# Filters and spectra of the long convolutions in column-scaled half-precision pairs, transform matrices used as loaded

## The chip, the cores and the metric

The kernel runs on one core of one Trainium2 chip. The core has five engines with a queue of instructions each: TensorE (PE in the profile; its weight loads are PEld), VectorE (DVE), ScalarE (ACT), GpSimd (POOL) and SyncE (SP), which here only issues transfers. The metric is the device time of one execution in microseconds (us), the median of three runs.

## The reference, cut to what matters

The model has two layers over 1024 latent tokens and 256 context tokens of width 1024. The first layer sends half of the channels through a Fourier transform, the other half through a gated long convolution (Hyena, order 2), whose filters come from a small network over positions:

```
def hyena_filters(L, w1, b1, freq, w2, b2, w3):
    ...
    h = jnp.sin(freq * (z @ w1 + b1))
    h = jnp.sin(freq * (h @ w2 + b2))
    h = (h @ w3).reshape(L, 2, HY_ORDER, HY_CH)
    ...
    h = h * jnp.exp(-t01 * deltas)[:, None, None, :]
    h = h / jnp.sum(jnp.abs(h), axis=(0, 1), keepdims=True)
    fwd, bwd = h[:, 0], h[:, 1]
    return jnp.concatenate([fwd, jnp.zeros_like(fwd[:1]), bwd[:0:-1]], axis=0)

def long_conv(u, filt, skip):
    ...
    ff = jnp.fft.rfft(filt, n=2 * L, axis=0)
    y = jnp.fft.irfft(uf * ff[None], n=2 * L, axis=1)[:, :L]
    return y + u * skip
```

Each column (channel, order) of the filter is divided by its own sum of absolute values, so a factor on a column of `w3` drops out of the result. There are two orders of 512 channels, and the filters are made for both lengths, 1024 ("l") and 256 ("c"), from the same weights. The second layer is neighbourhood attention; both layers end in a gated feed-forward part.

## The kernel before

One core does everything in one pass; activations lie with channels on the 128 partitions and tokens along the free axis, in tiles of 512 tokens. The program is written as Python generators whose steps are interleaved by hand; a planner then fixes the order on each engine from its own model of the instruction times, with buffers taken from pools of a fixed number of slots (20 of 4 KB per partition, 34 of 2 KB, two each of the tags `ws`, `wh`, `wl`, and eight banks of PSUM). An instruction queued behind a waiting one on its engine waits with it.

What is computed before the first projection:

- `filter_mlp` makes the hidden layer of the filter network for both lengths at once (640 columns), with a range reduction on VectorE before each sine, and splits the result into a rounded part and a remainder (`ta`, `tb`).
- `ada_first` (64 four-byte matmul instructions) makes two of the six modulations of layer 0 from sixteen 512 KB blocks of `ada_k`, loaded from POOL's queue into `wh`/`wl`.
- `filter_raw` loads the two directions of `w3` for an order, forms their sum and difference (L621), splits each into a high and a low part (helper `split`, L287 on ScalarE and L289 on VectorE), multiplies with `ta`/`tb` block by block, and multiplies the PSUM result with a decay tile `win` (L641), which SP loads in the step that uses it.
- `filter_spectrum` turns the raw filter of an order into its spectrum: four transform families i, four blocks b each. The nested generator `operands` combines the raw halves (L702 to L708), splits the combination, and fetches the transform matrix with `cmat`: a half-precision pair is loaded into a staging tile (tag `ws`) and cast on ScalarE (L335) to a four-byte tile (`wh`/`wl`). For every block and each of four output tiles, three matmuls follow: high × high, high × low, low × high. At the end of a family four PSUM tiles are evicted by ScalarE (L745) and stored by SP.
- `filter_sum`, advanced from within `filter_spectrum`, sums the absolute values over positions: two absolute values on ScalarE (L653, L654), a maximum (L655) and a running addition (L657) on VectorE, and 1-column matmuls that add over partitions.
- `norms` squares the rows of x and the context (ten 512 KB loads from SP, L2144), and normalises the transposed blocks (L550 to L553) as operands of the projection.

The order at the start: one step each of the network, the adaLN generator, the raw filter of order 0 and the norms, then the rest of the network, eight steps of adaLN, and the raw filter, whose VectorE and ScalarE instructions in its next step are tied behind the network's last clamp and sine. Raw filter 1 runs under spectrum 0, the norms under spectrum 1. Then `in_proj` begins; under its sixteen blocks run the 256-token filters (the same functions with "c", the sums and differences there on POOL) and 32 further adaLN steps.

Of the kernel before, what the change touches and what calls it, by code (L numbers as in the profile page):

```python
# [10 lines left out]
F32 = mybir.dt.float32  # L11
F32R = mybir.dt.float32r
F16 = mybir.dt.float16
# [188 lines left out]
class Builder:  # L202
# [117 lines left out]

    def cmat(self, w, src, view=None, small=False, shift=False):

        if small:
            st, m = self.S2(F16), self.S2(F32R, w)
            self.ld(view(st[:, :w]) if view else st[:, :w], src)
            self.nc.scalar.copy(m, st[:, :w])
            return m
        st = self.pw.tile([P, w], F16, tag="ws", name=self.nm("cs"))
        self.ld(view(st) if view else st, src)
        if shift:  # L330
            self.mk ^= 1
            m = self.shifted(("wh", "wl")[self.mk], "mat", w)
        else:
            m = self.mat(w)
        self.nc.scalar.copy(m, st)  # L335
        return m
# [224 lines left out]
    def filter_mlp(self):  # L561
# [12 lines left out]
        for layer, w in enumerate((w1, w2)):  # L574
            s = self.S4(F32, 640)
            for c0, cw in ((0, 512), (512, 128)):
                ps = self.PS()
                self.mm(ps[:, :cw], w, x[:, c0:c0 + cw], True, True)
                nc.vector.tensor_scalar(s[:, c0:c0 + cw], ps[:, :cw], vec[:, layer:layer + 1], vec[:, 2:3],
                                        op0=ADD, op1=MUL)  # L580
            n = self.S4(F32, 640)
# [6 lines left out]
            x = s  # L588
        self.tap("mlp", x)
        self.ta, self.tb = {}, {}  # L590
        for sq, c0, cw in (("l", 0, 512), ("c", 512, 128)):
            ta, tb = self.S2(F32R, cw), self.S2(F32R, cw)
            cs = slice(c0, c0 + cw)
            nc.scalar.copy(ta[0:64], x[0:64, cs])
            nc.vector.tensor_tensor(ta[64:128], x[0:64, cs], ta[0:64].bitcast(F32), SUB)
            nc.scalar.copy(tb[64:128], x[64:128, cs])
            nc.vector.tensor_tensor(tb[0:64], x[64:128, cs], tb[64:128].bitcast(F32), SUB)
            self.ta[sq], self.tb[sq] = ta, tb
        self.sgn = self.S2(F32R)
        self.ldr(self.sgn, a["sgn"][:, :512])  # L600
        self.alt = self.C(4, F32R)
# [3 lines left out]
        self.frg, self.rn, self.kap = {}, {}, {}  # L605

    def filter_raw(self, sq, raws, os=(0, 1)):
# [3 lines left out]
        w3, st = {}, {}  # L611
        for o in os:
            for j in (0, 1):
                st[(o, j)] = self.S2()
                self.ld(st[(o, j)], a["w3"][:, (2 * j + o) * HC:(2 * j + o + 1) * HC])
        if sq == "l":
            yield
        for o in os:
            for eo, op in ((0, ADD), (1, SUB)):
                t = self.T()  # L620
                (nc.vector if sq == "l" else nc.gpsimd).tensor_tensor(t, st[(o, 0)], st[(o, 1)], op)  # L621
# [23 lines left out]
    def filter_sum(self, sq, o, raw):  # L645
# [3 lines left out]
        if sq == "l":  # L649
            acc = self.S4()  # L650
            for b in range(nb):
# [4 lines left out]
                if b:  # L656
                    nc.vector.tensor_tensor(acc, acc, t, ADD)  # L657
# [21 lines left out]
    def filter_spectrum(self, sq, o, raw):  # L679
# [8 lines left out]
        fh = (self.S2(F32R), self.S2(F32R))  # L688
        nc.scalar.copy(fh[0][0:1, :], re[0:1, :])
        nc.vector.tensor_tensor(fh[1][0:1, :], re[0:1, :], fh[0][0:1, :].bitcast(F32), SUB)  # L690
# [5 lines left out]
        def operands():  # L696
            for i in range(4):
                for b in range(nb):
# [1418 lines left out]
    def run(self):  # L2117
# [11 lines left out]
        def drain(g):  # L2129
            for _ in g:  # L2130
                pass
# [60 lines left out]
        next(ng)  # L2192
        drain(mlp)
# [313 lines left out]
```

## Time and profile before

| | us |
|---|---|
| median of three runs | 2925.82 |
| the three runs | 2924.45 to 2926.82 |
| profiled execution | 2922.39 |
| its span | 2920.6 |
| mean granted clock of TensorE | 0.98 |

How to read it: the page lists the busy time of each engine, then the costliest groups of instructions, one line each: line of the kernel, engine, operation, output <- inputs with their shapes, count, busy time, mean duration in ns, and behind the second bar the engine's idle time just before them with what ended it ("releaser"). The timeline lists instructions in order of time: start, duration, instruction, and in brackets the idle time before. The list of waits says which engine waited for what: total, number, longest. The table by stretches gives, for each stretch from the span's start, the busy time of PE, PEld, DVE, ACT and POOL with the number of instructions, the granted clock of TensorE as a share of full speed, the share of the transfer engines and GB/s. Four-byte matmul operands, f32 and its faster form fp32r, both show as f32 on TensorE's rows.

### The profile page before, as it was taken

To read this page: it belongs to the slowest core of one execution; us is meant where nothing else is said; L and a number is where in the kernel's file an instruction comes from. 1 tells how busy PE (TensorE), PEld (TensorE's weight loads), DVE (VectorE), ACT (ScalarE), POOL (GpSimd) and SP (SyncE) were. 2 spreads that over 40 slices of the span, in tenths; PEclk is the share of its full clock that TensorE was granted. 3 is DMA by queue.
4 is the path that set the end of the run, shared out by engine and by line. 5 is a ranking of instruction groups with operands and counts; after the bars stand their busy time and mean duration, and the time that the engine had idled before them with its cause. 6 is when DMAs were issued, how large, how long until landed. Compare 5 with 4: busy or idle time off the path is not lost. (4 is left out here: it accounts for less than half of the span.)

```text
span 2920.6 us, 46051 instructions
## 1 busy us (share of the span) xinstructions
PE 2777.4 (95%) x16163; PEld 1710.9 (59%) x16163; DVE 2094.0 (72%) x3833; ACT 1647.9 (56%) x2899; POOL 641.4 (22%) x1057
## 2 busy tenths in 40 slices
PE   7889999999989999999999999999999999999998
PEld 3766557878879644444555844677665444444554
DVE  5678867585367798877886777777676778775765
ACT  4675325453675666654555555677664477654553
POOL 1012013354220111123120012454443022112000
PEclk9999999999999999999999999999999999999999
DMA  7574435358685555565995798777775666425753
GB/s 263 182 272 161 156 123 158 110 160 287 257 348 192 207 209 195 201 218 218 332 332 174 267 343 296 171 188 180 184 198 187 238 226 232 152 94 183 237 193 115
DMA packets 325156, 615.98 MB, mean 211 GB/s; under 512 B 90934, under 2 KB 130552, under 8 KB 324922
## 3 DMA queue, kind: packets, MB, share of 16 engines
q1 hardware_dynamic: 252378, 384.38, 40.4%
q0 software_dynamic: 70240, 224.45, 21.5%
q10 hardware_dynamic: 2304, 4.20, 0.4%
q8 instruction: 127, 2.08, 0.3%
q14 instruction: 107, 0.88, 0.1%
HBM read 455.33 MB, written 135.53 MB: 202 GB/s over the span
## 5 line engine op out<-in xcount | busy, mean ns | idle before, releaser
L1444 PE MATMUL ps<-s,s 128*128 128x512 f16 x2592 | 583.2, 382 | 15.8 <-ACT tk L1449 7.2
L1444 PEld LDWEIGHTS <-s 128*128 128x128 f16 x2640 | 258.9, 98 | 334.6 <-issue 30.3
L283 PE MATMUL ps<-s,wh 128*128 128x256 f32 (+3 forms) x1752 | 395.7, 329 | 13.1 <-ACT wh L287 7.3
L1213 ACT ACTIVATE s<-s,c 128x512 f16<-128x512 f32 (+1 forms) x324 | 233.3, 753 | 137.9 <-DMA s<-d 75.8
L1661 PE MATMUL ps<-s 128*128 128x512 f16 (+2 forms) x1308 | 305.0, 379 | 2.0 <-DVE s L1214 2.0
L1214 DVE SCALAR_TENSOR_TENSOR s<-s,c,s 128x512 f16<-128x512 f32 (+1 forms) x324 | 247.4, 794 | 78.3 <-ACT s L1213 77.7
L283 PE MATMUL pq<-s,wh 128*128 128x512 f16 (+1 forms) x1000 | 282.0, 356 | 12.2 <-DMA wh<-d 4.7
L283 PEld LDWEIGHTS <-wh 128*128 128x128 f16 x1664 | 160.3, 99 | 172.7 <-issue 24.7
L283 PE MATMUL ps<-s,wl 128*128 128x256 f32 (+3 forms) x876 | 260.2, 330 | 1.0 <-DVE wl L289 0.9
L274 POOL DMA_DIRECT2D d<-s x201 | 109.0, 543 | 660.5 <-DVE s L1505 193.1
L1661 PEld LDWEIGHTS <-s 128*128 128x128 f16 x1536 | 148.7, 98 | 179.5 <-issue 7.1
L283 PE MATMUL ps<-s,s 128*128 128x65 f16 (+5 forms) x2666 | 220.5, 235 | 20.2 <-DMA s<-s 8.2
L335 ACT CAST mat<-cs 128x1024 fp32r<-128x1024 f16 (+2 forms) x120 | 111.6, 935 | 139.0 <-PE ps L283 56.7
L283 PEld LDWEIGHTS ps<-s,wh 128*128 128x128 f32 x1088 | 178.0, 193 | 20.0 <-ACT wh L287 8.3
L283 PE MATMUL ps<-s,mat 128*128 128x512 f32 x696 | 182.8, 410 | 4.0 <-ACT s L287 3.0
L1444 PE MATMUL ps<-s,wh 128*128 128x512 f16 x616 | 185.0, 379 | 1.5 <-DVE g L1458 1.5
L283 PE MATMUL pq<-s,wl 128*128 128x512 f16 (+1 forms) x500 | 174.9, 355 | 1.6 <-DMA wl<-d 1.1
L283 PEld LDWEIGHTS <-s 128*128 128x128 f16 x2400 | 114.8, 98 | 79.5 <-DMA s<-s 9.1
L283 PEld LDWEIGHTS ps<-s,mat 128*128 128x128 f32 x696 | 135.4, 197 | 38.5 <-ACT s L287 4.4
L1246 ACT ACTIVATE t<-s 128x1024 bf16<-128x1024 f32 (+1 forms) x164 | 141.7, 866 | 14.4 <-DVE c L465 12.1
L1213 ACT ACTIVATE s<-t,c 128x512 f16<-128x512 f32 x172 | 115.1, 712 | 26.1 <-DVE c L1312 15.0
L283 PEld LDWEIGHTS ps<-s,s 128*128 128x128 f32 (+1 forms) x746 | 112.2, 190 | 27.6 <-DVE st L2039 4.2
(431 smaller groups left out, 5449.2 us busy)
## 6 DMA issues: line engine op xcount, KB each, us to landing
s<-d SPq DMA_DIRECT2D x294, 256.0 KB, 4.3
d<-s POOLq DMA_DIRECT2D x157, 256.0 KB, 3.2
s<-in_down SPq DMA_DIRECT2D x154, 256.0 KB, 5.4
s<-in_ada_w POOLq DMA_DIRECT2D x48, 512.0 KB, 5.0
g<-in_bias POOLq DMA_DIRECT2D x128, 192.0 KB, 3.3
s<-in_gate SPq DMA_DIRECT2D x46, 512.0 KB, 3.8
s<-in_up SPq DMA_DIRECT2D x46, 512.0 KB, 3.8
d<-g POOLq DMA_DIRECT2D x87, 256.0 KB, 3.0
```

The lines of the kernel that those rows point to most:

```text
L274: self.last_ldr = self.nc.gpsimd.dma_start(out, in_).ins
L283: self.nc.tensor.matmul(o, l, r, start=st, stop=sp)
L335: self.nc.scalar.copy(m, st)
L1213: nc.scalar.activation(hi, src, AF.Copy, scale=scale)
L1214: nc.vector.scalar_tensor_tensor(lo, src, scale, hi, op0=MUL, op1=SUB)
L1246: self.nc.scalar.activation(junk[:, :t.shape[1]], t, AF.Abs, scale=2.0 ** -15, accum_out=st[:, k:k + 1])
L1444: nc.tensor.matmul(ps, x[:, sl], y, start=first and j == 0 and x is wh and y is xh, stop=j == 3 and x is wl, skip_group_check=True)
L1661: m = nc.tensor.matmul(acc[j][:, c0:c1], x[:, sl], y[:, xs], start=first and k == 0, stop=last and k == 2, skip_group_check=True)
```

## The change

Five things are changed.

1. The pairs of the filter path become half precision: `ta`, `tb`, the sign rows, the parts of `w3` and of the spectrum's operands. A pair takes one tile of 1024 half-precision columns, where two four-byte tiles of 512 were used. The transform matrices, which lie in memory as half-precision pairs already, are loaded into a tile of one of the three tags in turn (`mat16`) and used as they are.
2. For the range of half precision, the columns of `w3` are scaled: absolute values in bf16 on ScalarE, their sum over the 128 rows on TensorE, a clamp and a reciprocal on VectorE, and one product for each of sum and difference. The scaled halves of the first use are stored to memory from POOL's queue, and the 256-token filters load them instead of forming them again.
3. Three of the eight decay tiles of an order are requested together with `w3`.
4. The running addition L657 goes from VectorE to POOL.
5. The network gets a step after the evictions of its first layer and one after its first sine, and the raw filter's two new steps are put there.

```diff
+    def mat16(self, w):
+        self.m16 = (getattr(self, "m16", 0) + 1) % 3
+        return self.pw.tile([P, w], F16, tag=("ws", "wh", "wl")[self.m16], name=self.nm("m16"))
...
+            if layer == 0:
+                yield
             n = self.S4(F32, 640)
...
             x = s
+            if layer == 0:
+                yield
...
-            ta, tb = self.S2(F32R, cw), self.S2(F32R, cw)
+            ta, tb = self.S2(F16, cw), self.S2(F16, cw)
...
+        self.w3d = {(o, eo): self.DR([P, 1024], F16) for o in (0, 1) for eo in (0, 1)}
+
+    def split16(self, src):
+
+        t = self.S2(F16, 1024)
+        self.last_hi = self.nc.scalar.copy(t[:, :512], src).ins
+        self.nc.vector.tensor_tensor(t[:, 512:], src, t[:, :512], SUB)
+        return t[:, :512], t[:, 512:]
...
-        if sq == "l":
+        w3, win = {}, {}
+        if sq == "c":
+            for key, d in self.w3d.items():
+                t = self.S2(F16, 1024)
+                self.ld(t, d)
+                w3[key] = (t[:, :512], t[:, 512:])
+        else:
+            st = {}
+            for o in os:
+                for j in (0, 1):
+                    st[(o, j)] = self.S2()
+                    self.ld(st[(o, j)], a["w3"][:, (2 * j + o) * HC:(2 * j + o + 1) * HC])
+            for b, k in ((0, 0), (0, 1), (1, 0)):
+                win[(b, k)] = self.S2()
+                self.ld(win[(b, k)], a["win_l"][b, k])
             yield
-        for o in os:
-            for eo, op in ((0, ADD), (1, SUB)):
-                t = self.T()
-                (nc.vector if sq == "l" else nc.gpsimd).tensor_tensor(t, st[(o, 0)], st[(o, 1)], op)
-                hi, lo = self.S2(F32R), self.S2(F32R)
-                self.split(t, hi, lo)
-                w3[(o, eo)] = (hi, lo)
+            sums = {}
+            for o in os:
+                ab = self.T(BF16, 1024)
+                ps = sums[o] = self.PS()
+                for j in (0, 1):
+                    nc.scalar.activation(ab[:, j * 512:j * 512 + 512], st[(o, j)], AF.Abs)
+                for j in (0, 1):
+                    self.mm(ps, self.ones.bitcast(BF16)[:, 1::2], ab[:, j * 512:j * 512 + 512], j == 0, j == 1)
+            yield
+            ts = {}
+            for o in os:
+                rec = self.T()
+                nc.vector.tensor_scalar(rec, sums[o], 1e-30, 2.0 ** -14, op0=MAX, op1=MUL)
+                nc.vector.reciprocal(rec, rec)
+                for eo, op in ((0, ADD), (1, SUB)):
+                    t = ts[(o, eo)] = self.S2()
+                    nc.vector.tensor_tensor(t, st[(o, 0)], st[(o, 1)], op)
+                    nc.vector.tensor_tensor(t, t, rec, MUL)
+            yield
+            for key, t in ts.items():
+                w3[key] = self.split16(t)
+                for j in (0, 1):
+                    self.ldr(self.w3d[key][:, j * 512:j * 512 + 512], w3[key][j])
...
-                w = self.S2()
-                self.ld(w, a["win_" + sq][b, s])
+                w = win.pop((b, s), None)
+                if w is None:
+                    w = self.S2()
+                    self.ld(w, a["win_" + sq][b, s])
...
-                    nc.vector.tensor_tensor(acc, acc, t, ADD)
+                    nc.gpsimd.tensor_tensor(acc, acc, t, ADD)
...
-                    xh, xl = self.S2(F32R), self.S2(F32R)
-                    self.split(t, xh, xl)
-                    yield xh, xl, self.cmat(2 * nb * P, a["ff_" + sq][i, b])
+                    xh, xl = self.split16(t)
+                    mt = self.mat16(2 * nb * P)
+                    self.ld(mt, a["ff_" + sq][i, b])
+                    yield xh, xl, mt
...
         next(fr)
         next(ng)
+        next(mlp)
+        next(fr)
+        next(mlp)
+        next(fr)
         drain(mlp)
```

More of the change, by code (lines that the diff above doesn't have):

```diff
@@ L591, in filter_mlp @@
         for sq, c0, cw in (("l", 0, 512), ("c", 512, 128)):
[L592 removed]
+            ta, tb = self.S2(F16, cw), self.S2(F16, cw)
             cs = slice(c0, c0 + cw)
             nc.scalar.copy(ta[0:64], x[0:64, cs])
[L595 removed]
+            nc.vector.tensor_tensor(ta[64:128], x[0:64, cs], ta[0:64], SUB)
             nc.scalar.copy(tb[64:128], x[64:128, cs])
[L597 removed]
+            nc.vector.tensor_tensor(tb[0:64], x[64:128, cs], tb[64:128], SUB)
             self.ta[sq], self.tb[sq] = ta, tb
[L599 removed]
+        self.sgn = self.S2(F16)
         self.ldr(self.sgn, a["sgn"][:, :512])
[L601 removed]
+        self.alt = self.C(4, F16)
         self.ldr(self.alt, a["sgn"][:, 512:516])
@@ L687, in filter_spectrum @@
         nc.vector.tensor_scalar(f0[0:1, :], f0[0:1, :], 0.5, None, op0=MUL)
-        fh = (self.S2(F32R), self.S2(F32R))
+        fh = self.S2(F16, 1024)
+        fh = (fh[:, :512], fh[:, 512:])
         nc.scalar.copy(fh[0][0:1, :], re[0:1, :])
-        nc.vector.tensor_tensor(fh[1][0:1, :], re[0:1, :], fh[0][0:1, :].bitcast(F32), SUB)
+        nc.vector.tensor_tensor(fh[1][0:1, :], re[0:1, :], fh[0][0:1, :], SUB)
         m0, m1 = self.mask[:, 0:1], self.mask[:, 1:2]
```

5 lines of the change are left out of this document (removed).

## The prediction

> **What bounds the kernel now.** I read the page first, for the engines over the whole span, and then cut the span at the places where the changed code runs: up to 200.7 us the filters of the 1024-token stream, their spectra and the normalisations are made; from there on the input projection runs, with the 256-token filters woven in.
>
> ```profile
> PE 2777.4 (95%) x16163; PEld 1710.9 (59%) x16163; DVE 2094.0 (72%) x3833; ACT 1647.9 (56%) x2899; POOL 641.4 (22%) x1057
> ...
> 20.00:80.00 60.00, 58.26 (x196) 25.26 (x195) 34.37 (x72) 33.77 (x60) 7.32 (x14) 1.00 0.61 226
> 80.00:140.00 60.00, 52.31 (x209) 41.78 (x209) 41.13 (x70) 40.58 (x62) 0.00 (x0) 0.89 0.59 193
> 140.00:200.70 60.70, 52.17 (x215) 39.67 (x214) 46.71 (x72) 49.66 (x75) 1.28 (x2) 0.94 0.68 231
> 200.70:285.00 84.30, 82.58 (x463) 49.41 (x463) 67.88 (x139) 39.37 (x79) 22.41 (x24) 0.96 0.56 204
> ```
>
> Columns after the length are PE, PEld, DVE, ACT, POOL, granted clock, DMA share. TensorE bounds the kernel, and in the part that changes too: from 20 to 80 us it idles 1.7 us, from 80 to 200.7 us 16.2 us, and there the clock is below 1. So a gain has to come out of TensorE's gaps, its slow clock, or the spacing of its matmuls. The gaps, in order of time:
>
> ```profile
> 82.87 0.79 PE L283 MATMUL pq<-s,s 128*128 128x512 f32 x1 [1.96 <-ACT s L287]
> 121.70 3.35 PE L283 MATMUL ps<-c,s 128*128 128x1 f32 x16 [3.05 <-DVE s L657]
> 137.05 0.39 PE L283 MATMUL ps<-s,c 128*2 128x512 f32 x1 [2.68 <-ACT s L287]
> 159.81 5.63 PE L283 MATMUL ps<-s,mat 128*128 128x512 f32 x17 [2.69 <-ACT s L287]
> 188.09 7.69 PE L283 MATMUL ps<-s,mat 128*128 128x512 f32 x32 [0.96 <-DVE s L289]
> 200.65 0.16 PE L283 MATMUL pq<-st,c 128*128 128x2 bf16 x1 [4.87 <-DVE st L1295]
> ```
>
> Four of the six wait for the high or low half of a spectrum operand (L287, L289): 1.96 + 2.68 + 2.69 + 0.96 = 8.3 us. Why is that half late? ScalarE before the first of them:
>
> ```profile
> 78.59 1.05 ACT L335 CAST mat<-cs 128x1024 fp32r<-128x1024 f16 x1 [2.20 <-PE pq L283]
> 80.25 1.56 ACT L745 COPY s<-ps 128x512 f32<-128x512 f32 x3 [0.62 <-PE ps L283]
> 82.17 1.17 ACT L287 CAST s<-tk 128x512 fp32r<-128x512 f32 x2
> ...
> L335 ACT CAST mat<-cs 128x1024 fp32r<-128x1024 f16 x32 | 33.4, 1049 | 30.2 <-issue 13.7 <-PE ps L283 12.6 <-PE pq L283 2.2
> ...
> SPq L268 <- ACT mat L335: 91.7, 27, 24.2
> ```
>
> The cast of a transform matrix (L335) waits for a buffer that TensorE still reads; the evictions and the split sit behind it, and SP's queue stands 91.7 us behind these casts (27 waits).
>
> **The change, part by part.** Its time is made against the profiled execution's own, 2922.4 us (span 2920.6 and 1.8 around it), 3.4 us under the median of 2925.82; I add the sum to the median.
>
> *Casts gone.* All 32 L335 casts up to 200.7 us go, 33.4 us of ScalarE with 30.2 us of waiting ahead of them. The matrix is loaded into one of six slots (two each of three tags, as many as staging and matrices had), so the wait for TensorE moves to SP's queue. What is queued there behind it: decay tiles, rows of x, the spectra's stores; they stood behind the casts already. A high/low pair now takes one small buffer, not two, which lets splits run further ahead. Bounds: 0 (splits still stand behind four evictions, about 2.2 us) and the whole 8.3. I take **−6**, nearer the upper, because at 78.59 the queue stands 2.20 us on a cast, not on the splits' inputs.
>
> *Slow clock after those gaps.*
>
> ```profile
> 80.00:85.00 5.00, 3.04 (x9) 1.99 (x9) 1.86 (x4) 4.75 (x10) 0.00 (x0) 0.60 0.80 289
> 85.00:90.00 5.00, 5.00 (x18) 3.93 (x17) 3.60 (x7) 1.46 (x2) 0.00 (x0) 0.72 0.75 238
> 120.00:125.00 5.00, 3.30 (x17) 3.30 (x17) 5.00 (x10) 3.00 (x6) 0.00 (x0) 0.70 0.23 87
> 125.00:130.00 5.00, 5.00 (x15) 3.97 (x15) 5.00 (x15) 1.05 (x1) 0.00 (x0) 0.62 0.20 52
> 155.00:160.00 5.00, 2.31 (x8) 1.50 (x7) 4.65 (x5) 5.00 (x9) 0.00 (x0) 0.84 0.32 124
> 160.00:165.00 5.00, 5.00 (x16) 3.98 (x17) 5.00 (x9) 3.52 (x6) 0.00 (x0) 0.71 0.94 322
> ```
>
> The clock column is the last but two. Around 82.87 and 159.81 it loses (0.40 + 0.28 + 0.16 + 0.29) × 5 = 5.7 us; the gaps lie partly inside, so **−4**, between 0 and −5.7. The Trainium skill ("TensorE: Matmul & The Clock Gate", "Part 1: The HAM clock gate") has the array throttled after an idle window of about 3.4 us. Taken literally, no gap here is long enough, and this term would be 0 and the forecast 4 us later; the trace does not agree, since the clock falls to 0.60 beside a gap of 1.96 us.
>
> *Half-precision matmuls.* The burst at 188.09 has 32 matmuls of four-byte operands in 7.69 us; with a last one of 0.39 that is 7.30 / 31 = 0.2355 us from one to the next. Half-precision ones of the same shape:
>
> ```profile
> 1010.51 7.93 PE L1444 MATMUL ps<-s,s 128*128 128x512 f16 x36
> ...
> L283 PE MATMUL ps<-s,mat 128*128 128x512 f32 x288 | 81.8, 421 | 3.7 <-ACT s L287 2.7 <-DVE s L289 1.0
> L283 PE MATMUL pq<-s,mat 128*128 128x512 f32 x96 | 27.9, 403 | 0.0
> ```
>
> (7.93 − 0.38) / 35 = 0.2157 us. The two spectra have 288 + 96 = 384 such matmuls, the raw filters 64 (4 blocks × 2 halves × 2 × 2, for each of two orders): 448 × 0.0198 = 8.9 us. Where TensorE waits for operands it gains nothing, so **−6.5**, between 0 and −8.9.
>
> *Column scaling.* Per order ScalarE gets two absolute values (0.6 us each by the splits at 82.17), TensorE two matmuls, VectorE one clamp, a reciprocal over 512 columns and two products.
>
> ```profile
> L675 DVE RECIPROCAL c<-c 128x4 f32<-128x4 f32 x2 | 0.3, 171 | 0.0
> L2146 DVE RECIPROCAL c<-c 128x10 f32<-128x10 f32 x1 | 0.2, 216 | 4.3 <-ACT c L2145 4.3
> L687 DVE TENSOR_SCALAR t<-t 1x512 f32<-1x512 f32 x1 | 0.4, 404 | 0.0
> L708 DVE TENSOR_TENSOR t<-s 128x512 f32<-128x512 f32 x24 | 16.1, 682 | 0.0
> L657 DVE TENSOR_TENSOR s<-s,s 128x1024 f32<-128x1024 f32 x6 | 7.3, 1216 | 0.0
> ...
> 18.53 1.13 DVE L579 TENSOR_SCALAR s<-ps,c 128x512 f32<-128x512 f32 x2 [2.94 <-PE ps L283]
> 18.85 7.37 PE L283 MATMUL ps<-mat,c 128*2 128x512 f32 x16
> ```
>
> No reciprocal of that width stands in the trace: 0.7 us if it runs like the sum of two tensors, 0.17 + 508 × 0.0075 = 4.0 us by the slope of the two rows above (45 ns over six columns). I take 4.0, because the rows are of this very operation. An order then costs VectorE 0.4 + 4.0 + 2 × 0.68 = 5.8 us. The first order's falls into the filter network, where VectorE is free for 2.94 us ahead of 18.53; the two operand sums (2 × 0.68) move ahead of it too, so the network is late by 0 to 5.8 + 1.4 − 2.9 = 4.3 us. Cover: the 16 adaLN matmuls that hold TensorE from 18.85 to 26.2. I take **+1.5**. The second order's lies under spectrum 0, where VectorE is free for 60 − 41.1 = 18.9 us: nothing, if that cover holds (the second rival).
>
> *Decay tiles early.*
>
> ```profile
> 5.71 10.71 SPq L268 DMA_DIRECT2D s<-in_x_row  x10
> 22.33 7.65 SPq L268 DMA_DIRECT2D s<-in_win_l  x6
> 33.95 0.69 DVE L641 TENSOR_TENSOR s<-ps,s 128x512 f32<-128x512 f32 x1 [5.21 <-DMA s<-in_win_l]
> ```
>
> Three of the tiles now go ahead of ten 512 KB rows of x, which get 0.75 MB later. VectorE's 5.21 us go, but TensorE idles only 1.7 us from 20 to 80, so **−1**, between 0 and −1.7. What is late next is the scaled matrix itself.
>
> *Sum over positions.* Six additions (L657, 7.3 us of VectorE) go to POOL, which has nothing else to do there.
>
> ```profile
> L274 POOL DMA_DIRECT2D mat<-in_ada_k x16 | 8.5, 534 | 40.4 <-PE ps L283 38.1 <-DMA mat<-in_ada_k 2.3
> ...
> L896 POOL TENSOR_TENSOR t<-t,t 128x512 f32<-128x512 f32 x40 | 53.7, 1360 | 72.5 <-DVE t L895 70.7 <-ACT s L287 1.3
> 115.02 2.35 DVE L655 TENSOR_TENSOR s<-s,s 128x1024 f32<-128x1024 f32 x2
> 206.06 6.39 POOL L621 TENSOR_TENSOR t<-s,s 128x512 f32<-128x512 f32 x4 [26.02 <-DMA s<-in_w]
> 208.02 1.10 DVE L289 TENSOR_TENSOR s<-t,s 128x512 fp32r<-128x512 f32 x1 [1.82 <-ACT s L287]
> ```
>
> Twice the width costs at most 2 × 1.6 = 3.2 us by L621; I take 2 × 1.36 = 2.7. The sum's matmuls at 121.70 wait for the last one. The third and fourth maxima are there at 116.2 and 117.4 (L655 at 115.02), and nothing stands ahead of POOL's additions: two of them end at 116.2 + 5.4 = 121.6, at 3.2 each 1 us later, at VectorE's own 1.2 us three earlier. I take **0**, between −3 and +1.
>
> *The 256-token filters* read the stored halves: four POOL additions (6.39 us), four splits and eight small casts go. Under the projection TensorE is busy 82.58 of 84.30 us, so **−1**, between 0 and −1.7; eight stores pay for it on POOL's queue, 0.53 us each to issue like the adaLN loads above, and those loads stand 40.4 us waiting there anyway.
>
> Sum: −6 − 4 − 6.5 + 1.5 − 1 + 0 − 1 = **−17**, so 2925.8 − 17 = **2909 us**, with its own range 2901 to 2916.
>
> **The rivals.**
> *The wait only changes its place.* SP's queue waits for the slots, the evictions still stand ahead of the splits. For it: six slots before and after. Against it: a load needs no turn on ScalarE. Gaps and clock stay, spacing is lost in the waits; about −3, so 2923.
> *VectorE becomes the bound.* From 140 to 200.7 us it is already busy 46.7 of 60.7. It gets 2 × 5.8 − 7.3 = +4.3 us, and POOL's additions, 6 × 2.7 = 16 us, lengthen its two-input operations: 0.68 to 1.10 at 208.02, a loss of 0.38 of the time, 6 us. It decides once VectorE's free time in a spectrum is gone: operands then pace TensorE, the −16.5 of gaps, clock and spacing is lost, and +10 remains: 2936. Against it: 19 us free from 80 to 140. The Trainium skill ("SBUF — State Buffer", "Who interferes with whom") has a VectorE operation with two SBUF inputs blocked for the whole of a GpSimd operation that reads SBUF; by that up to 16 us would be lost instead of 6, 2946. The row at 208.02 bears out the conflict, and a smaller price.
> *More than the sum.* The freed ScalarE also closes the gap at 121.70 with its clock (3.05 + (0.30 + 0.38) × 5 = 6.4 us) and the 4.87 us ahead of the projection, where ScalarE works through evictions: 2925.8 − 17 − 11 = 2898.
> *Half precision is not faster here.* The spacing comes from elsewhere; without the 6.5: 2916.
>
> **How the numbers follow.** Forecast 0.47, more than the sum 0.17, spacing unchanged 0.06, wait moved 0.14, VectorE bound 0.16. The range 2894 to 2931 takes in all but the far parts of the third and of the second. A measurement of this kernel tells 0.2%, 5.9 us, from no change. Faster: 0.47 + 0.17 + 0.06 = 0.70; same 0.14; slower 0.16. All instructions behind the projection keep their work, but their order is planned from modelled times for the whole program, so stretches that the edit does not touch may move by a few us either way; the range holds that too.
>
> **What would show it.** No L335 under "mat<-cs" before the convolutions; gaps on L287's successor under 3 us in all; granted clock 1.0 from 80 to 95 us; a burst of 32 matmuls in about 7.1 us; a reciprocal of about 4 us at the front; the projection's first matmul about 16 us before 200.65. The forecast is wrong if that comes at the same time, if VectorE is busy over 95% from 80 to 185 us, or if the time is lost again after it.

## The result, and the profile after

| | before | after |
|---|---|---|
| median of 12 runs on one chip, us | 2925.57 | 2923.77 |
| lowest to highest, us | 2915.98 to 2929.75 | 2913.00 to 2929.57 |
| ratio, 95% interval | | 0.9991 [0.9978, 1.0004] |
| profiled execution, us (its span) | 2922.39 (2920.6) | 2927.05 (2925.3) |
| the projection's first matmul, us from the start | 200.65 | 205.50 |

The change makes no difference that can be measured. Single executions of one kernel spread over 14 to 17 us, so the medians decide, and the two profiled ones are compared only stage by stage. Behind the filter part every line number of after is 45 higher; the split of a pair is L619 (ScalarE) and L620 (VectorE), where it was L287 and L289.

The page of after, its first row, the engines over the span:

```profile
PE 2771.2 (95%) x16167; PEld 1664.3 (57%) x16167; DVE 2103.0 (72%) x3831; ACT 1614.5 (55%) x2859; POOL 657.5 (22%) x1067
```

TensorE's work fell by 6 us and ScalarE's by 33 us (the casts), and the end did not move. The stretches of after, with the columns that the prediction names:

```profile
0.00:20.00 20.00, 3.64 (x6) 1.30 (x6) 7.09 (x11) 2.76 (x4) 3.90 (x13) 1.00 0.88 316
20.00:80.00 60.00, 53.15 (x165) 15.07 (x166) 33.67 (x69) 27.18 (x55) 9.92 (x18) 1.00 0.68 236
80.00:140.00 60.00, 52.48 (x242) 22.78 (x241) 50.24 (x78) 28.93 (x50) 9.77 (x7) 0.99 0.59 200
140.00:200.70 60.70, 52.65 (x221) 21.58 (x220) 51.22 (x72) 34.60 (x54) 9.83 (x5) 0.89 0.58 192
200.70:285.00 84.30, 76.90 (x436) 44.66 (x436) 60.70 (x130) 39.24 (x77) 16.41 (x20) 0.94 0.58 218
...
80.00:85.00 5.00, 5.00 (x23) 1.74 (x22) 2.16 (x6) 0.00 (x0) 0.00 (x0) 1.00 0.15 54
85.00:90.00 5.00, 5.00 (x23) 1.73 (x21) 0.00 (x0) 1.08 (x3) 0.00 (x0) 1.00 0.35 107
165.00:170.00 5.00, 3.98 (x10) 1.43 (x10) 5.00 (x9) 0.75 (x1) 0.00 (x0) 0.50 0.14 52
```

From 80 to 140 us the change did what it was expected to do: ScalarE's 40.6 us have become 28.9, the clock 0.89 has become 0.99, and TensorE gets through 242 matmuls where it had 209. From 140 us on the clock is 0.89, where it was 0.94. And from 20 to 80 us TensorE, busy for 58.26 us before, is busy for 53.15 with 165 matmuls instead of 196: a loss in the stage where almost nothing was left to gain. TensorE's larger gaps in after (start, duration, instruction, idle time before it and what ended it):

```profile
13.05 1.22 PE L283 MATMUL ps<-t,c 128*128 128x512 bf16 x2 [4.16 <-ACT t L648]
25.03 2.50 PE L283 MATMUL ps<-s,t 128*128 128x512 f32 x4 [10.75 <-ACT s L593]
27.46 10.02 PE L283 MATMUL ps<-mat,c 128*2 128x512 f32 x20
...
125.26 1.95 PE L283 MATMUL ps<-c,s 128*128 128x1 f32 x16 [0.89 <-POOL s L700]
136.25 0.38 PE L283 MATMUL pq<-s,c 128*2 128x512 f16 x1 [1.84 <-ACT s L619]
139.53 1.44 PE L283 MATMUL ps<-s,m 128*128 128x512 f16 x3 [1.93 <-ACT s L619]
161.12 0.81 PE L283 MATMUL ps<-s,m 128*128 128x512 f16 x3 [0.88 <-ACT s L619]
166.01 2.72 PE L283 MATMUL ps<-s,m 128*128 128x512 f16 x6 [3.87 <-DVE s L620]
184.99 2.75 PE L283 MATMUL ps<-s,m 128*128 128x512 f16 x12
205.50 0.16 PE L283 MATMUL ps<-st,c 128*128 128x2 bf16 x1 [7.86 <-DVE st L1340]
```

A gap of 10.75 us stands at 25.03: the second layer of the filter network waits for the first sine (L593). The adaLN matmuls, which were the cover in the prediction and began at 18.85 us before, are queued on TensorE behind this very instruction and begin at 27.46, 8.6 us later. VectorE's queue says why the sine is late:

```profile
13.09 1.30 DVE L659 TENSOR_TENSOR s<-s,s 128x512 f32<-128x512 f32 x2 [12.07 <-DMA s<-in_w]
14.30 1.12 DVE L583 TENSOR_SCALAR s<-ps,c 128x512 f32<-128x512 f32 x2
15.34 0.68 DVE L655 TENSOR_SCALAR t<-ps 128x512 f32<-128x512 f32 x1
15.94 0.48 DVE L588 TENSOR_SCALAR s<-s 128x640 f32<-128x640 f32 x1
16.34 3.35 DVE L656 RECIPROCAL t<-t 128x512 f32<-128x512 f32 x1
19.60 0.43 DVE L589 TENSOR_SCALAR s<-s 128x640 f32<-128x640 f32 x1
19.94 1.28 DVE L660 TENSOR_TENSOR s<-s,t 128x512 f32<-128x512 f32 x2
21.14 2.54 DVE L591 SCALAR_TENSOR_TENSOR s<-s,s 128x640 f32<-128x640 f32 x3
...
27.15 1.13 DVE L583 TENSOR_SCALAR s<-ps,c 128x512 f32<-128x512 f32 x2 [2.94 <-PE ps L283]
```

The sum and difference of `w3` (L659) stand ahead of the network's evictions (L583) and wait for the transfer of `w3` until 13.09; with them ahead, the evictions come at 14.30. In the kernel before they came 4.0 us earlier, and they too waited for a transfer:

```profile
10.30 1.13 DVE L579 TENSOR_SCALAR s<-ps,c 128x512 f32<-128x512 f32 x2 [9.28 <-DMA c<-in_mlpv]
```

Then the clamp, the reciprocal and the products (L655, L656, L660) stand between the steps of the network's range reduction, 0.68 + 3.35 + 1.28 = 5.3 us. From the first eviction to the sine it now takes 24.24 − 14.30 = 9.9 us, where it took 15.63 − 10.30 = 5.3. Two things therefore add up to the 8.6 us: 4.0 behind a transfer at the head of the queue, and 4.6 for the scaling in the middle of it.

The order in which the kernel is written does not put them there. Its steps make sum, difference, clamp, reciprocal and products behind the first sine; the planner, which fixes the order on each engine, moved them ahead of it. The last row shows what is left open: VectorE still waits 2.94 us ahead of the second evictions, the gap in which the prediction had the scaling run.

### The profile page after: what moved, and what is told of

It reads as the page before. It is cut to its first block, busy times and chain, and to the rows that moved or that the text cites. A ratio compares the mean times of both kernels' runs of the same rounds, so it can differ in the third digit from the quotient of the medians.

```text
span 2925.3 us, 46020 instructions
## 1 busy us (share of the span) xinstructions
PE 2771.2 (95%) x16167; PEld 1664.3 (57%) x16167; DVE 2103.0 (72%) x3831; ACT 1614.5 (55%) x2859; POOL 657.5 (22%) x1067
## 5 line engine op out<-in xcount | busy, mean ns | idle before, releaser
L1489 PEld LDWEIGHTS <-s 128*128 128x128 f16 x2640 | 258.1, 98 | 330.4 <-issue 23.7
L283 PE MATMUL ps<-s,wh 128*128 128x256 f32 (+3 forms) x1848 | 407.6, 327 | 9.3 <-ACT wh L287 7.3
L283 PE MATMUL ps<-s,wl 128*128 128x256 f32 (+3 forms) x924 | 268.5, 327 | 0.9 <-DVE wl L289 0.9
L283 PE MATMUL pq<-s,wh 128*128 128x512 f16 (+1 forms) x904 | 258.6, 365 | 7.6 <-DMA wh<-d 2.9
L1706 PEld LDWEIGHTS <-s 128*128 128x128 f16 x1536 | 148.5, 98 | 179.4 <-issue 7.1
L283 PEld LDWEIGHTS <-s 128*128 128x128 f16 x2500 | 124.1, 98 | 100.5 <-issue 17.5
L283 PE MATMUL pq<-s,wl 128*128 128x512 f16 (+1 forms) x452 | 161.4, 365 | 2.1 <-DMA wl<-d 2.1
L1291 ACT ACTIVATE t<-s 128x512 bf16<-128x512 f32 (+1 forms) x166 | 143.9, 868 | 7.7 <-DMA s<-in_w_in 2.1
L283 PEld LDWEIGHTS <-wl 128*128 128x128 f16 x832 | 82.3, 99 | 79.1 <-issue 4.8
L339 ACT CAST mat<-cs 128x1024 fp32r<-128x1024 f16 (+2 forms) x80 | 74.9, 943 | 92.0 <-PE ps L283 37.9
L1259 DVE SCALAR_TENSOR_TENSOR s<-t,c,s 128x512 f16<-128x512 f32 x172 | 123.3, 745 | 1.0 <-ACT s L1258 1.0
L1489 PE MATMUL ps<-s,wl 128*128 128x512 f16 x308 | 116.5, 379 | 0.0
```

Source lines behind the costliest of these rows:

```text
L283: self.nc.tensor.matmul(o, l, r, start=st, stop=sp)
L1259: nc.vector.scalar_tensor_tensor(lo, src, scale, hi, op0=MUL, op1=SUB)
L1291: self.nc.scalar.activation(junk[:, :t.shape[1]], t, AF.Abs, scale=2.0 ** -15, accum_out=st[:, k:k + 1])
L1489: nc.tensor.matmul(ps, x[:, sl], y, start=first and j == 0 and x is wh and y is xh, stop=j == 3 and x is wl, skip_group_check=True)
L1706: m = nc.tensor.matmul(acc[j][:, c0:c1], x[:, sl], y[:, xs], start=first and k == 0, stop=last and k == 2, skip_group_check=True)
```

## The experiments

All ratios are against the kernel before on the same chip: e1 to e4 ran on one chip, e5 to e8 on a second, e9 to e11 on a third, so that differences between these groups are differences of ratios. The last column is the projection's first matmul in the one profiled execution of each run, 200.65 us in the kernel before. The first theory (A): the removed casts bring what was forecast, and the column scaling, placed ahead of the network, takes it back. Its rivals: POOL's additions take it back through VectorE (B); the order planned for the later stages decides, and the end does not follow the front (C); or the casts were never worth anything.

| run | what it is | median, us | ratio [95%] | projection, us |
|---|---|---|---|---|
| e1 | after, scaling behind the network | 2928.15 | 1.0002 [0.9989, 1.0015] | 205.46 |
| e2 | after, addition on VectorE | 2924.90 | 0.9993 [0.9982, 1.0005] | 204.17 |
| e3 | e1 and e2 together | 2924.12 | 0.9991 [0.9977, 1.0004] | 201.51 |
| e4 | e1's order, no scaling | 2916.19 | 0.9959 [0.9944, 0.9974] | 193.65 |
| e5 | e2, scaling in VectorE's gap | 2916.79 | 0.9961 [0.9945, 0.9976] | 201.00 |
| e6 | e3, first order unscaled | 2918.33 | 0.9963 [0.9948, 0.9978] | 194.34 |
| e7 | e3, no order scaled | 2913.04 | 0.9949 [0.9933, 0.9965] | 198.68 |
| e8 | before, early decay tiles alone | 2922.51 | 0.9990 [0.9977, 1.0003] | 199.94 |
| e9 | e7, matrices copied by ScalarE again | 2927.42 | 0.9997 [0.9984, 1.0010] | 200.71 |
| e10 | e7 and two edits | 2911.81 | 0.9942 [0.9925, 0.9959] | 192.08 |
| e11 | e5 and the same two edits | 2917.32 | 0.9960 [0.9945, 0.9975] | 199.02 |

### e1: the two new steps of the raw filter behind the whole network

```diff
-        next(mlp)
-        next(fr)
-        next(mlp)
-        next(fr)
         drain(mlp)
...
         with self.tc.issue_after(self.clamp), self.tc.issue_after(self.sin):
-            next(fr)
+            for _ in range(3):
+                next(fr)
```

> Edit: the changed kernel with the raw filter's two new steps put behind the whole filter network again (tied behind its last clamp and sine) instead of between its layers. Theory A (the late network ate the gain): TensorE's second network matmul starts near 16.4 us again instead of 25.03, the wait of 10.75 us ahead of it falls to about 7.2, the projection's first matmul comes 6 to 9 us before the 205.50 of the changed kernel, and the time is 6 to 9 us under its 2923.8, near 2916. Theory B (VectorE, held by POOL's additions, is the bound from 90 us on): the front moves, but the projection starts within 2 us of 205.5 and the time stays at 2922 to 2925. Theory C (the order planned for the later stages decides): the projection starts earlier and the end does not follow.

The network's matmul is back at 16.41 behind a wait of 7.68 us, as theory A had it, but the projection (205.46) does not come 6 to 9 us earlier and the time did not fall: 1.0002 [0.9989, 1.0015]. TensorE's timeline of e1, its two gaps ahead of 50 us:

```profile
16.41 2.50 PE L283 MATMUL ps<-s,t 128*128 128x512 f32 x4 [7.68 <-ACT s L593]
...
45.18 1.83 PE L283 MATMUL ps<-c,g 2*128 2x2 f32 x8 [6.54 <-ACT g L430]
```

and ScalarE's timeline of e1, between the two:

```profile
32.95 1.22 ACT L619 CAST s<-s 128x512 f16<-128x512 f32 x2 [5.54 <-DVE s L660]
34.08 1.05 ACT L2189 ACTIVATE s<-s 128x1024 f32<-128x1024 f32 x1
...
43.44 1.04 ACT L2189 ACTIVATE s<-s 128x1024 f32<-128x1024 f32 x1
44.48 1.03 ACT L430 COPY g<-ps 2x512 f32<-2x512 f32 x2
```

The scaling now delays the split of `w3` (L619, waiting 5.54 us for the product L660). The ten squares of the norms (L2189) are tied behind the last split, and the adaLN row copy (L430) is queued on ScalarE behind all ten; TensorE waits 6.54 us for it. The stretches of e1 show the clock there:

```profile
40.00:45.00 5.00, 0.00 (x0) 0.00 (x0) 0.00 (x0) 5.00 (x12) 0.00 (x0) 0.64 0.48 193
45.00:50.00 5.00, 4.82 (x12) 2.12 (x12) 2.35 (x5) 4.62 (x13) 0.00 (x0) 0.50 0.00 2
```

So e1 does not refute that the scaling costs the time; it moves the place where it is paid. The simple form of the theory, that its place ahead of the network alone is the cost, falls.

### e2 and e3: the running addition back on VectorE

```diff
-                    nc.gpsimd.tensor_tensor(acc, acc, t, ADD)
+                    nc.vector.tensor_tensor(acc, acc, t, ADD)
```

e2 has this edit alone, e3 has it and e1's.

> Edit: the changed kernel with the running addition of the filter sums back on VectorE. Theory B: the six additions cost VectorE 7.3 us again, but the operations that stood behind POOL (about 2 us each time) are short again, about 10 us; the gap of 3.87 us at 166 us closes with the slow clock behind it, the projection starts 4 to 8 us earlier than 205.5 and the time falls by as much, to 2916 to 2920. Theory A: nothing at the front changes (network matmul at 25.0), the projection within 2 us of 205.5, the time within 3 us of 2923.8.

> Edit: both of the edits before together. Theories A and B each hold and add: projection 12 to 15 us earlier than 205.5, time 2909 to 2912, which is the time forecast for the change. If only A holds, as the network-first kernel; if only B, as the kernel with the addition on VectorE. Theory C: the projection starts early and the time does not follow.

e2 is at 0.9993, e3 at 0.9991; after was at 0.9991 and e1 at 1.0002. Where the addition runs changes the time by −3 to +1 us (0.9991 − 1.0002 and 0.9993 − 0.9991, times 2926), inside the intervals; e7 against e4, below, gives −3 again. The projection comes 1.3 us earlier in e2 and 4.0 in e3, not 4 to 8 and 12 to 15. The rival that POOL's additions take the gain back falls as the main cause; a cost of some 3 us is not excluded. The conflict itself is there. POOL's group in after, by lines:

```profile
L700 POOL TENSOR_TENSOR s<-s,s 128x1024 f32<-128x1024 f32 x6 | 16.0, 2661 | 57.6 <-DVE s L698 57.6
```

The timeline of after around three of the six, POOL and VectorE:

```profile
158.07 2.79 POOL L700 TENSOR_TENSOR s<-s,s 128x1024 f32<-128x1024 f32 x1 [32.87 <-DVE s L698]
158.66 3.28 DVE L698 TENSOR_TENSOR s<-s,s 128x1024 f32<-128x1024 f32 x1
162.09 2.72 POOL L700 TENSOR_TENSOR s<-s,s 128x1024 f32<-128x1024 f32 x1 [1.23 <-DVE s L698]
162.53 2.83 DVE L750 SCALAR_TENSOR_TENSOR tk<-s,c 128x512 f32<-128x512 f32 x1
173.19 3.04 POOL L700 TENSOR_TENSOR s<-s,s 128x1024 f32<-128x1024 f32 x1 [8.39 <-DVE s L698]
174.04 2.74 DVE L752 TENSOR_TENSOR t<-s 128x512 f32<-128x512 f32 x1
```

L752 takes 2.74 us here; before, as L708, it took 0.68. Each of the three VectorE operations begins within POOL's and ends 0.5 to 1.1 us behind it. Beside the other three additions, from 114 to 126 us, L620 (twice) and L698 lengthen in the same way, by 2.2, 1.2 and 1.2 us; with 2.1 each for the three shown, that is 10.8 us for the six.

### e4, e6, e7: without the scaling

In e4 and e7 no column of `w3` is scaled, in e6 only those of the second order are; sums, clamp, reciprocal and products are left out. All three stand in e1's order; e6 and e7 add on VectorE, e4 on POOL. The edit of e4 and e7, beside e1's:

```diff
-            sums = {}
-            for o in os:
...
-            yield
             ts = {}
             for o in os:
-                rec = self.T()
-                nc.vector.tensor_scalar(rec, sums[o], 1e-30, 2.0 ** -14, op0=MAX, op1=MUL)
-                nc.vector.reciprocal(rec, rec)
                 for eo, op in ((0, ADD), (1, SUB)):
...
-                    nc.vector.tensor_tensor(t, t, rec, MUL)
```

and that of e6, beside e3's:

```diff
-            for o in os:
+            for o in os if os != (0,) else ():
...
-                nc.vector.reciprocal(rec, rec)
+                if o in sums:
...
+                    nc.vector.reciprocal(rec, rec)
...
-                    nc.vector.tensor_tensor(t, t, rec, MUL)
+                    if o in sums:
+                        nc.vector.tensor_tensor(t, t, rec, MUL)
```

> Edit: the network-first kernel without the column scaling (no absolute values, sums, clamp, reciprocal, products; sum and difference are split to half precision unscaled; the additions stay on POOL). Prices the scaling away from the network: VectorE loses 2 x 5.3 us of work. If the scaling lies under other work there, within 2 us of the network-first kernel; if VectorE is the bound (theory B), 4 to 10 us faster than it.

> Edit: network first, addition on VectorE, column scaling left out for order 0 alone and kept for order 1, where it runs under spectrum 0. Theory A2: it gains nearly all of what leaving the scaling out gains, projection 194 to 196 us, time 2914 to 2918. Theory B2: half of it, projection near 198, time near 2920.

> Edit: the kernel without scaling, with the addition back on VectorE as well. If POOL's additions cost there what they cost the network-first kernel (about 4 us), projection near 190 us and time 2911 to 2914; if the gap ahead of the projection, which SP's queue of loads sets, takes it up, within 2 us of 2916.

e7, e6 and e3 are a ladder of one written order and one place of the addition: no scaling 0.9949, second order scaled 0.9963, both 0.9991. Both orders together cost 0.0042 × 2926 = 12.3 us (6 to 18 by the intervals), with the intervals of e7 and e3 apart. The first order's share is 8 us and the second's 4 us; the steps in between have intervals that touch or overlap, so the division is not sharp. e4 against e1, with the addition on POOL, gives the same: 0.0043, 12.6 us, more than the 4 to 10 named for a bound on VectorE and far from the 2 named for a scaling that lies under other work. Against e2, where the scaling stands in the place that it has in after, e7 gains 0.0044, 12.9 us. This is the cost that takes the gain back.

Where in the execution it is paid is less clear. The start of the projection, from which the expectations worked, is met in e6 (194 to 196) and missed in e7, which starts it at 198.68 and not near 190, and all the same has the time that was expected; e6's time lies between its two theories. Of the 12.3 us between e3 and e7, 201.51 − 198.68 = 2.8 stand at the projection; the rest comes behind it.

### e5: the scaling kept, in VectorE's free time

The clamp and the reciprocal are tied behind the network's first clamp and run while ScalarE makes the first sine and TensorE the second layer; absolute values and their column sums run before that, at 12.27 and 12.95. The sum, difference and products are tied behind the last clamp and sine. Nothing is left out, and the addition is on VectorE.

```diff
+                recs[o] = rec
+            yield
+            for o in os:
+                rec = recs[o]
                 for eo, op in ((0, ADD), (1, SUB)):
...
         next(mlp)
-        next(fr)
         next(mlp)
-        next(fr)
+        with self.tc.issue_after(self.clamp):
+            next(fr)
+            next(fr)
         drain(mlp)
...
             next(fr)
+            next(fr)
```

> Edit: the changed kernel with the addition on VectorE and the first order's scaling moved: the column sums go behind the first sine, clamp and reciprocal into VectorE's idle 2.9 us while TensorE and ScalarE work on the network's second layer, sum, difference and products behind the last clamp. Theory A2 (the scaling's place ahead of the first raw matmul is what costs, 8.6 us when it delays the network, some 6 us when it follows it): the network is about 1 us late, the second network matmul at 16 to 17.5 us, the first halves of w3 1 to 3 us later than without scaling; the projection 4 to 8 us earlier than the 201.3 of the kernel with both edits, time 2914 to 2918. Theory B2 (the scaling costs as VectorE work, wherever it stands): the projection and the time stay within 2 us of that kernel, 2922 to 2926.

e5 computes all that after does and is at 0.9961 [0.9945, 0.9976], apart from e2's 0.9993 [0.9982, 1.0005], of which it is a reordering: 9.4 us. TensorE's timeline of e5:

```profile
16.50 2.50 PE L283 MATMUL ps<-s,t 128*128 128x512 f32 x4 [2.33 <-ACT s L593]
```

and VectorE's:

```profile
10.39 1.13 DVE L583 TENSOR_SCALAR s<-ps,c 128x512 f32<-128x512 f32 x2 [9.38 <-DMA c<-in_mlpv]
...
15.60 0.68 DVE L655 TENSOR_SCALAR t<-ps 128x512 f32<-128x512 f32 x1
16.32 3.35 DVE L656 RECIPROCAL t<-t 128x512 f32<-128x512 f32 x1
19.59 1.03 DVE L583 TENSOR_SCALAR s<-ps,c 128x512 f32<-128x512 f32 x2
```

The first evictions are back at 10.39 and the second layer's matmul at 16.50 instead of 25.03. Clamp and reciprocal fill the time in which VectorE waited 2.94 us before; the second evictions come at 19.59, against 18.53 in the kernel before. A network that is 1 us late is what the prediction's +1.5 meant, and it takes this order to get it. The time is as expected, the projection is not: 201.00, where 4 to 8 us less than 201.3 was written, so that most of the 9.4 us, too, shows only behind it.

### e8 and e9: the other parts alone

e8 is the kernel before with nothing but the three early decay tiles.

```diff
+            for b, k in ((0, 0), (0, 1), (1, 0)):
+                win[(b, k)] = self.S2()
+                self.ld(win[(b, k)], a["win_l"][b, k])
```

> Edit: the kernel before with nothing changed but the three decay tiles requested together with w3. Prices that part alone: VectorE's wait of 5.21 us at 33.95 goes; TensorE, busy 58.3 of 60 us there, gains 0 to 1.7 us, so the time stays within 2 us of the kernel before. If the raw filter's start sets the pace of the front, the projection comes 3 to 5 us earlier.

0.9990 [0.9977, 1.0003], −2.9 us with zero inside the interval; −1 was forecast. The projection comes 0.7 us earlier, not the 3 to 5 of the case that the raw filter's start sets the pace.

e9 is e7 (no scaling) with the transform matrices again loaded into a staging tile and copied by ScalarE, half precision to half precision. Only the removal of the casts is undone.

```diff
-                    mt = self.mat16(2 * nb * P)
-                    self.ld(mt, a["ff_" + sq][i, b])
+                    cs = self.pw.tile([P, 2 * nb * P], F16, tag="ws", name=self.nm("cs"))
+                    self.ld(cs, a["ff_" + sq][i, b])
+                    mt = self.mat(2 * nb * P, F16)
+                    nc.scalar.copy(mt, cs)
```

> Edit: the kernel without scaling and with the addition on VectorE, but each transform matrix is staged and copied by ScalarE again as in the kernel before (to a half-precision tile); pairs stay half precision. Splits the forecast's gain: if the casts and the gaps they cause were worth the 10 us forecast (gaps and clock), it is 8 to 12 us slower than the same kernel without the copies (2913), near 2923; if the spacing of the half-precision matmuls carries the gain, it stays within 4 us, at 2913 to 2917, and bursts keep 0.216 us from matmul to matmul.

The gain is gone: 0.9997 [0.9984, 1.0010] against 0.9949 [0.9933, 0.9965] for e7, 14.0 us (8 to 20 by the intervals), where 8 to 12 was expected. The group of copies in e9, by lines:

```profile
L744 ACT COPY mat<-cs 128x1024 f16<-128x1024 f16 x32 | 33.4, 1044 | 35.6 <-PE ps L283 21.6 <-PE pq L283 6.7 <-issue 4.4
```

32 copies of 1.04 us with 35.6 us of waiting ahead of them, as before (33.4 and 30.2), and SP's list of waits in e9 up to 201 us is headed, as that of before was, by the wait for the copies:

```profile
SPq L268 <- ACT mat L744: 64.3, 25, 6.1
```

TensorE's timeline of e9, where the matmuls are half precision:

```profile
121.68 1.01 PE L283 MATMUL pq<-s,mat 128*128 128x512 f16 x2 [5.14 <-DVE s L620]
...
186.62 7.93 PE L283 MATMUL ps<-s,mat 128*128 128x512 f16 x36
```

The last row is (7.93 − 0.38) / 35 = 0.2157 us from one matmul to the next, just what was forecast; but e9, with all its half-precision matmuls, is not faster than before: the gap at 121.68 is 5.14 us where it was 3.05 at 121.70, so that part of what the matmuls save is waited for again. In all, TensorE waits 12.8 us in e9 for the halves of the operands from 80 to 201 us. In e7 the list of waits for that stretch still has most of it:

```profile
PE ps L283 <- ACT s L619: 3.6, 2, 2.4
PE ps L283 <- DVE s L620: 3.1, 3, 2.3
PE pq L283 <- DVE s L620: 2.9, 2, 1.7
```

These 9.6 us are no less than the 8.3 of the kernel before, and at the projection e7 is only 2.0 us ahead of e9. So closed gaps are not what makes e7 faster. More of it is in the clock: the mean granted clock over the whole execution is 0.9817 in e7 and 0.9784 in e9, as the mean of their six and twelve executions; the kernel before has 0.9795 and 0.9794 on the two chips. Span × (1 − clock), an estimate of what the slow clock costs, is 53 and 63 us, 10 of the 13 us between the means of their times. Between e1 and e4, whose clocks are 0.9798 and 0.9800, it differs by less than 1 us: the cost of the scaling is not the clock's.

### e10 and e11: two more edits

The squares are tied behind the adaLN row copies instead of the last split, and the matrices of the 256-token filters take small tiles. e10 adds this to e7 (so it has no scaling), e11 to e5.

```diff
-                    mt = self.mat16(2 * nb * P)
+                    mt = self.mat16(2 * nb * P) if sq == "l" else self.S2(F16, 2 * nb * P)
...
-            with self.follow(self.last_hi):
+            with self.follow(self.rowcopy):
```

> Edit: the kernel without scaling and with the addition on VectorE, with the squares of the norms tied behind the adaLN row copies on ScalarE (instead of behind the split of w3), and the 256-token matrices in small tiles of their own, so that their loads don't stand for a big slot in SP's queue ahead of the projection's weights. Should end TensorE's wait of 2.9 us at 40 us with its slow clock (2 to 4 us) and bring the projection's first weights 2 us earlier: 2908 to 2911. If the front's stream of adaLN blocks sets the pace, the first does nothing; if ScalarE's work ahead of the projection does, the second does nothing: 2913.

> Edit: the same two further edits on the kernel that keeps the scaling in VectorE's gap (addition on VectorE). 2 to 5 us under its 2916.8, so 2912 to 2915, and faster than the kernel before beyond noise with everything kept that the change computes.

Neither shows a gain over what it stands on, and both miss their forecasts, e10 narrowly: 0.9942 [0.9925, 0.9959] against 0.9949, and 0.9960 [0.9945, 0.9975] against 0.9961. e10 starts the projection 6.6 us earlier than e7, and its end does not follow. e10 is the fastest of all, but without scaling it lacks the protection of the half-precision range. Of the versions that compute all, e5 and e11 are the best; their intervals lie clear of 1 and just clear of that of after.

## Why the prediction was right or wrong

The time, 2923.8, lies in the range and misses the forecast of 2909 and its own range. The sum went wrong in one term above all, and the other large terms came out near their sum without the mechanism that they were made from.

**The step that failed: column scaling, +1.5 with bounds 0 and +4.3, and nothing for the second order.** e7, e6 and e3 put it at 12.3 us for both orders. What failed first is the place. The prediction had the first order's scaling run in the 2.94 us for which VectorE is free ahead of 18.53, behind the second layer's matmul. In after the planner put it ahead of the first sine; that gap is still there at 27.15, and the second layer itself is 8.6 us late. The cover, "the 16 adaLN matmuls that hold TensorE from 18.85 to 26.2", fails with the place: in TensorE's queue these matmuls stand behind the second layer, so they cover what is late behind it, but a late first sine delays them too. The second fault was to price only the instructions. The prediction said that the two operand sums move ahead, but not that they wait there for `w3` until 13.09 with the network's first evictions queued behind them (14.30 instead of 10.30), and it did not ask who is behind a late split of `w3`. In the place that the prediction meant, e5, the price was near: the scaling costs 0.0012 × 2926 = 3.5 us over e7, with overlapping intervals.

**Casts gone −6, slow clock −4, half-precision matmuls −6.5.** The sum came near. e7, which has these three and the two terms of −1 each, is at −14.9 (0.0051 × 2926; −10.2 to −19.6 by its interval), where the forecast has −18.5 without the scaling. That is in part luck, for the terms one by one did not come. With the copies kept, e9 should have had −8.5 from the spacing and the two small terms, and has −0.9 (−4.7 to +2.9); taking the copies away brings 14.0 and not 10. The −6 stood for shorter waits for an operand's halves, 8.3 us before; they are 9.6 in e7 and 6.5 + 2.8 + 1.8 = 11.1 in after. And the −4 was made from the clock beside two gaps ahead of the projection, whereas most of what separates e7 from e9 shows behind it. What e9 shows is that staging and copying the matrices on ScalarE costs the time; it brings back the copies, their waits and the smaller number of slots that a load can go into together, so which of them costs it, and why the clock is the better for it, stays open. No run took the casts away while keeping the four-byte matmuls.

**Decay tiles −1 and the 256-token filters −1.** e8 fits the first. The second was not tried alone; e9 holds both, and is at −0.9 in all.

**Sum over positions 0, between −3 and +1.** The time fits (e2, e3). The sum's matmuls wait 0.89 us for L700 at 125.26, where they waited 3.05 us for L657 before. One step of the working is off: the conflict of the additions with VectorE was underpriced, as the second rival shows.

**The rivals.** The first, that the wait only changes its place, has the right time, 2923, for the wrong reason. SP's list of waits in after, up to 201 us, does show the new place:

```profile
SPq L268 <- PE ps L283: 43.2, 15, 7.8
SPq L268 <- DMA mat<-in_ada_k: 27.4, 2, 19.4
SPq L268 <- PE pq L283: 26.9, 10, 4.9
```

70 us of waiting for a slot that TensorE reads stand where 91.7 us on casts stood, and 27 us more are put down to the adaLN blocks, whose tiles share two of the three tags: SP waits as long as before. But nothing of ScalarE's is behind these waits, and e7, which has them as well, gains its 14.9 us. The second, VectorE as the bound: it is busy for 50.24 of 60 us and 51.22 of 60.7, 84%, not the 95% that was named, and e2 takes POOL's additions away without gain. The prediction's 6 us for six additions was too little: they lengthen VectorE's operations by 10.8 us in all. By the Trainium skill ("SBUF — State Buffer", "Who interferes with whom"), a VectorE operation with two inputs in SBUF is blocked by a POOL operation that reads SBUF and has begun first, until that is through; as an estimate from this and the 16.0 us of POOL's group, up to 16 us could be lost. The trace agrees with the blocking, since VectorE's operations end 0.5 to 1.1 us behind POOL's beside all six; the loss stays smaller, as they begin up to 1 us after POOL's. e2 shows no time for it; that VectorE had it to spare is the likely reason, not a tested one. The third, more than the sum: the gap ahead of the projection grew from 4.87 to 7.86 us instead of closing.

**What would show it.** No cast of a transform matrix is left, the clock is 1.00 from 80 to 90 us, a burst runs at (2.75 − 0.38) / 11 = 0.2155 us, and the reciprocal takes 3.35 us. Not met: TensorE's waits for L619 are still 1.84 + 1.93 + 0.88 = 4.6 us, with 3.87 us for L620 at 166.01 and a clock of 0.50 around it, and the projection comes 4.9 us later instead of 16 earlier. That last sign pointed to the front of the kernel, 25 us in, before any spectrum runs.

**What was not settled.** In the profiled execution of after the lag against before changes sign and comes back behind the projection, in stages that the edit does not touch; with the spread between executions, no cause is claimed for it. Theory C has no experiment of its own. By the traces, VectorE and ScalarE run what stands behind the projection in the same order in after and in e5, but for under 1% of it, and e5 is 8.8 us faster (0.9991 − 0.9961), so that gain needs no other plan. Between e3 and e7 the order there differs in some 8% of VectorE's instructions, most of them before 500 us, and between e7 and e9 in some 3%. So a part of the 12.3 and of the 14.0 us may come from the plan.

## What to carry to other kernels

Work put on an idle engine's queue is hidden only if it neither waits there nor stands ahead of the instruction that the bound engine needs next: follow each cover in the queue's order, not in the trace's order of time. A planner may move it to another place than the one in which it is written; tie it there, as e5 does, if the price depends on the place. When an instruction waits for a buffer, price what is queued behind it on its engine; 33 us of copies on an engine busy for half of the time were worth 14 us of the end, though not by the gaps that one would list. A cost moved by reordering may reappear at the next thing tied to it, so look for who waits for the new last instruction before you call the place the cause. And an earlier start of a stage is not yet an earlier end: e10 gained 6.6 us at the projection and nothing clear of noise at the end.

## What was not expected of the hardware

Clamp, reciprocal and product of a scaling differ much in price. The group of reciprocals in after, by lines:

```profile
L656 DVE RECIPROCAL t<-t 128x512 f32<-128x512 f32 x2 | 6.7, 3340 | 0.0
```

3.34 us over 512 columns, against 0.68 us for the clamp of the same shape at 15.34: five times as much, and less than the 4.0 us drawn from two small reciprocals. And a VectorE operation of 0.68 us that begins beside a POOL addition of 3.04 us ends behind it, at 2.74 us; L684, which reads one of its inputs from PSUM, keeps its 0.68 us at 123.24, beside the addition from 122.86 to 125.20.

The granted clock carries much of the spread between executions of one kernel: the shortest of the twelve of after, 2913.00 us, has a mean clock of 0.985, the longest, 2929.57, of 0.980, which by the same estimate is 15 of the 17 us.
